# A decoder layer on one core: one load queue with x's first chunk ahead, whole rows of the adaLN weights, sums of squares on TensorE

## The chip, the core and the metric

The kernel runs on one core of a Trainium2 chip. TensorE multiplies, VectorE, ScalarE and GpSimd work on tiles in SBUF and PSUM, and each engine runs its own instructions in the order in which they were emitted. DMAs are issued by SyncE, ScalarE or GpSimd; a queue issues in order, and all share 16 DMA engines. The metric is the device time of one execution in microseconds, the median of several; one execution is profiled.

## The reference

One layer of a decoder for two groups of requests that share weights: a prompt of 1024 tokens, and 8 samples of 8 new tokens each with a paged cache of 4096. D is 1024, all is float32.

```python
mod = (jax.nn.silu(c) @ w_ada + b_ada)[:, None, :]
shift1, scale1, gate1, shift2, scale2, gate2 = jnp.split(mod, 6, axis=-1)
h = rms_norm(x, norm1) * (1 + scale1) + shift1
z = h @ w_in
...
k_cmp = rms_norm(compress(full[:, :, 0], cmp_pe[0], cmp_w1[0], cmp_w2[0]), k_gain[0])
v_cmp = compress(full[:, :, 1], cmp_pe[1], cmp_w1[1], cmp_w2[1])
o_cmp, p_cmp = cmp_attention(q, k_cmp, v_cmp, q_pos)
...
x = x + gate1 * (jnp.concatenate([o_attn, y_conv, y_pool], axis=-1) @ w_out)
h = rms_norm(x, norm2) * (1 + scale2) + shift2
x = x + gate2 * swiglu(h, w_up, w_down)
```

`compress` takes blocks of 32 raw keys or values with a step of 16, adds a position term, and applies a first weight, silu and a second weight. `c` is one vector for the prompt and one for each sample. The change edits how `mod`, the first `h` and the order of the first `compress` calls come about, not what is computed.

## The kernel before

Features lie on the 128 partitions, in KT = 8 tiles; the 1088 tokens (1024 of the prompt, then 64 of the samples) lie along the free axis in three chunks of 384, 384 and 320 (`CHUNKS`). Products of token data and weights are made from parts: an operand is split into `hi` and `lo`, and `mm3` (L142) issues three matmuls.

The program has three phases. **Phase 1** holds
- `ada_rounds` (L339): the six vectors of `mod`. Vectors 0 (shift) and 1 (scale) come first, from 32 loads (`wada`, 256 KB each, 16 buffers); vectors 2 to 5 come late, among the projection (`late_ada`, L899). A step takes 4 loads and 16 fp32 matmuls; a vector's half is then copied (`ada_s`), transposed and added to the bias.
- `norm_load`, `norm_squares`, `modulate` (L435, L441, L404) for each chunk: load of x, sum of its squares, then `h_hi` and `h_lo`. ScalarE makes the squares, VectorE adds the eight tiles, one fp32 matmul with `mean_d` sums over the partitions.
- `token_part` (L672): 9 token tiles by 24 matmuls with the 280 columns of `wtok`. It needs all 8 tiles of its chunk's `h`.
- `input_projection` (L833): 16 tiles of 128 output columns, each three chunks by 24 matmuls. Tiles kc and vc come first, q0 to q3 last; `head_norm` (L700) takes the keys and queries through a mean of squares (`h_sq`, `mean_h`), a root on ScalarE and a reciprocal on VectorE.
- `compress` (L498) for the sample caches: a batch has 4 octets of 8 pages; an octet is 8 loads of 128 KB in a `stream` tile and 16 matmuls, each two records in the trace. There are three `stream` tiles (L475); the first holds the first compression weights for good, two turn, and octet i+2 is loaded when octet i is done. `compress_post` (L575) closes a batch: silu, second weights (`c_w`), norm. The first three batches (EARLY) are spawned with phase 1; the other 20 octets run in phase 2.
- `compress_prompt` (L549): the same for the prompt's 1024 tokens, from `kcv`. ScalarE copies them into a `stream` tile in eight pieces; it waits for the three early batches.

`key_stacks` (L903) then splits the prompt's keys into `kh` (ScalarE) and `kl` (VectorE), from the 64 compressed keys (`kcp`) and the 1024 raw ones (`ksw`). **Phase 2** is attention with the rest of the compression, **phase 3** the output projection and the FFN.

What sets the order: tasks are generators with a priority; `run` (L83) emits the next step of the task with the least priority number among those whose time has come by a rough clock that the code keeps for each engine (`use`, L73). A change of costs, holds or priorities can so reorder all engines far behind it. In `build` (L1951) the front and the projection have priority 1, the early compression 2.

In before, SyncE's queue carries `wada`, the compression weights and the cache pages; ScalarE's queue x and `wtok`.

Of the kernel before, what the change touches and what calls it, by code (L numbers as in the profile page):

```python
# [17 lines left out]
P = 128  # L18
# [42 lines left out]
class Kernel:  # L61
# [84 lines left out]
    def evac(self, out, in_, n, ready=None):  # L146
        """PSUM to SBUF on the engine that is free first; the time at which it is there"""
# [7 lines left out]
    def combine(self, out, a, b, op, n, ready=0.0, eng=None):  # L155
        """out = a op b in SBUF on VectorE or GpSimd, by default the one that is done first"""
# [25 lines left out]
    # ---------------------------------------------------------------- constants  # L182
# [60 lines left out]
    def constants3(self, c):  # L243
        nc = self.nc
        with self.pool("ctmp") as tp:
# [9 lines left out]
            # zeros, then the causal triangle; the window's older edge; the compressed blocks that are not over yet  # L255
# [15 lines left out]
            # row index -> token t of a sample row (b2, g, r, t)  # L271
# [7 lines left out]
            # sum over the four heads of a key group  # L279
# [12 lines left out]
            # new tokens: key (b', t') is seen by row (b, t) when b' == b and t' <= t  # L292
# [11 lines left out]
            # the oldest window keys: key k is out of the window of token t when k <= t  # L304
# [6 lines left out]
            # token partition (64 + (b, t)) -> row (b2, g, r, t) of the pair p  # L311
# [8 lines left out]
            # head of a sample row  # L320
# [10 lines left out]
    # ---------------------------------------------------------------- adaLN  # L331
# [7 lines left out]
    def ada_rounds(self, pool, rs, bufs, eng, tag, margin=0.0):  # L339
        """vectors rs of the modulation, [feature, (prompt, 8 batches)], half a vector at a time"""  # L340
        nc = self.nc
        todo = [(r, hf) for r in rs for hf in range(2)]
        steps = [(x, kh) for x in range(len(todo)) for kh in range(2)]
        W = {}

        def load(i):
            if i < len(steps):
                x, kh = steps[i]
                r, hf = todo[x]
# [9 lines left out]
        for i in range(ahead):  # L359
            load(i)  # L360
        for i, (x, kh) in enumerate(steps):
            r, hf = todo[x]
            yield W[i][4] + margin
            if kh == 0:
# [7 lines left out]
            if kh == 0:  # L372
                continue
            s = pool.tile([P, P], F32, name="ada_s", bufs=2)
            r_ = self.evac(s, acc[:, :P], P)
# [3 lines left out]
            self.tr(tr[:, :P], s)  # L379
            nc.vector.tensor_tensor(  # L380
                self.mod[:, r].rearrange("p (g j) b -> p j g b", j=2)[:, hf],
                tr[:, :P].rearrange("p (g m) -> p g m", m=32)[:, :, 0:9],
                self.bada[:, r].rearrange("p (g j) -> p j g", j=2)[:, hf][:, :, None].to_broadcast([P, 4, 9]),
                op=OP.add)
            self.give(tag, self.use("dve", 0.2, self.t["pe"]))
            if hf == 1:
                if r in (1, 4):
                    out, norm = (self.s1, self.norm1) if r == 1 else (self.s2, self.norm2)
                    nc.vector.scalar_tensor_tensor(out, self.mod[:, r], 1.0, norm[:, :, None].to_broadcast([P, KT, 9]),
                                                   op0=OP.add, op1=OP.mult)  # L390
                self.ada_at[r] = self.use("dve", 0.3, self.t["pe"]) + 0.2
# [1743 lines left out]
```

## Time and profile before

| | us |
|---|---|
| median of 3 runs | 1713.56 |
| the runs | 1712.5, 1713.56, 1716.59 |
| span of the profiled execution | 1707.9 |
| TensorE busy | 1606.5 |
| VectorE busy | 1121.0 |
| ScalarE busy | 821.8 |
| GpSimd busy | 704.6 |

The span runs from the first to the last instruction of one execution; the run's time holds some microseconds around it. A row of a timeline is a run of like instructions with its start, its length, and in brackets how long the engine idled ahead of it and what released it. A group's row has a count, the busy time and the mean of one. Matmuls overlap in the records, so that a mean of 0.29 us stands for starts 0.13 us apart.

### The profile page before, as it was taken

How to read it: one execution, taken by the hardware profiler on the slowest of the kernel's cores; microseconds unless marked ns; L12 is line 12 of the kernel's file. 1: busy time of each engine (PE TensorE's matmuls, PEld its weight loads, DVE VectorE, ACT ScalarE, POOL GpSimd, SP SyncE). 2: the span in 40 equal slices, each digit the busy share in tenths (PEclk: the TensorE clock that was granted, in tenths of full speed). 3: DMA queues.
4: the chain of work that ended last, by engine and by line, in shares of the span. 5: the costliest groups of instructions: out<-in, count | busy, mean ns of one | idle time of the engine just before them, and what ended most of it. 6: DMA issues, size and time to landing. Idle time of an engine off the chain costs nothing.

```text
span 1707.9 us, 35277 instructions
## 1 busy us (share of the span) xinstructions
PE 1606.5 (94%) x12317; PEld 1427.7 (84%) x12317; DVE 1121.0 (66%) x2886; ACT 821.8 (48%) x1892; POOL 704.6 (41%) x812
## 2 busy tenths in 40 slices
PE   6789999997999999999799789999999999899998
PEld 5689999987877566666599779999999998889997
DVE  1491334767556867666599996555555556998887
ACT  1363212326676766766675543332333334655554
POOL 1121000003342322222206486555555555888976
PEclk9899999999999999999999989999999999999999
DMA  9854455425664644540883224225222225744433
GB/s 273 258 180 127 143 141 138 136 75 179 202 193 128 195 141 122 160 131 10 276 253 105 75 72 135 96 96 194 97 96 100 96 96 186 237 128 130 133 82 125
DMA packets 214851, 245.13 MB, mean 144 GB/s; under 512 B 25985, under 2 KB 182850, under 8 KB 214354
## 3 DMA queue, kind: packets, MB, share of 16 engines
q1 hardware_dynamic: 190546, 209.77, 40.1%
q10 hardware_dynamic: 18288, 17.01, 3.2%
q0 software_dynamic: 5840, 16.10, 2.9%
q8 instruction: 98, 1.61, 0.4%
q14 instruction: 79, 0.65, 0.1%
HBM read 202.33 MB, written 44.67 MB: 145 GB/s over the span
## 4 chain that ended last, share of the span: by engine, by line
PE 31%; DVE 9%; issue 4%; DMA 3%; POOL 3%; ACT 1%; ACTq 0%; POOLq 0%; DVEq 0%; SPq 0%
PE bank L135 31%; DVE w_lo L160 2%; DMA w_raw<-in_wup 2%; POOL w_s L160 1%; DVE b_lo L160 1%; DVE g_lo L160 1%; DVE x L1706 1%; DVE d_lo L160 1%; POOL b_t L160 1%; DMA w_raw<-in_wdown 0%; DMA mixc<-mix_d 0%; ACT w_hi L164 0%; DMA x<-x_d 0%; DVE n_ss L160 0%; POOL f_T L160 0%
## 5 line engine op out<-in xcount | busy, mean ns | idle before, releaser
L135 PE MATMUL bank<-b_lo,w_hi 128*128 128x272 f32 x1232 | 355.8, 291 | 2.7 <-DVE b_lo L160 2.5
L135 PE MATMUL bank<-b_hi,w_hi 128*128 128x272 f32 x1232 | 351.6, 292 | 6.9 <-DVE f_v L1512 3.3
L135 PE MATMUL bank<-b_hi,w_lo 128*128 128x272 f32 x1232 | 351.4, 290 | 2.1 <-DVE w_lo L160 2.1
L135 PEld LDWEIGHTS bank<-b_hi,w_hi 128*128 128x128 f32 x1232 | 232.1, 191 | 9.6 <-ACT b_hi L164 4.9
L135 PEld LDWEIGHTS bank<-b_lo,w_hi 128*128 128x128 f32 x1232 | 234.5, 190 | 4.0 <-DVE b_lo L160 3.9
L135 PEld LDWEIGHTS bank<-b_hi,w_lo 128*128 128x128 f32 x1232 | 233.0, 190 | 3.1 <-DVE w_lo L160 2.8
L160 POOL TENSOR_TENSOR w_s<-w_raw 128x512 f32<-128x512 f32 (+1 forms) x122 | 164.2, 1347 | 147.8 <-DVE w_lo L160 134.1
L1011 POOL TENSOR_SCALAR P<-P,st 128x640 f32<-128x640 f32 (+11 forms) x192 | 111.5, 591 | 241.8 <-DVE st L1009 89.5
L164 ACT ACTIVATE w_hi<-w_raw 128x512 fp32r<-128x512 f32 (+2 forms) x130 | 86.5, 676 | 176.5 <-PE bank L135 141.2
L160 DVE TENSOR_TENSOR w_lo<-w_raw,w_hi 128x512 fp32r<-128x512 f32 (+2 forms) x129 | 115.6, 904 | 83.2 <-PE bank L135 47.4
L160 DVE TENSOR_TENSOR w_lo<-w_s,w_hi 128x512 fp32r<-128x512 f32 (+1 forms) x144 | 127.4, 888 | 45.4 <-ACT w_hi L164 38.6
L135 PE MATMUL bank<-stream 128*128 128x128 f32 x1056 | 137.2, 289 | 19.4 <-DMA stream<-in_cacheA 14.5
L135 PEld LDWEIGHTS bank<-stream 128*128 128x128 f32 x1056 | 130.4, 203 | 28.5 <-issue 21.8
L160 POOL TENSOR_TENSOR x<-x,d_m 128x272 f32<-128x272 f32 x144 | 141.1, 1001 | 25.2 <-DVE x L1706 13.1
L164 ACT ACTIVATE w_hi<-w_s 128x512 fp32r<-128x512 f32 (+1 forms) x144 | 89.2, 624 | 113.2 <-PE bank L135 57.1
L135 PE MATMUL bank<-h_hi,w_hi 128*128 128x384 f32 (+1 forms) x384 | 129.4, 337 | 1.0 <-ACT py L826 1.0
L135 PE MATMUL bank<-h_hi,w_lo 128*128 128x384 f32 (+1 forms) x384 | 126.7, 330 | 0.0
L135 PE MATMUL bank<-h_lo,w_hi 128*128 128x384 f32 (+1 forms) x384 | 126.4, 329 | 0.0
L1003 ACT ACTIVATE P<-P,st 128x640 f32<-128x640 f32 (+11 forms) x192 | 113.0, 591 | 13.0 <-DVE st L994 6.5
L135 PE MATMUL bank<-g_hi,w_hi 128*128 128x272 f32 x308 | 92.0, 301 | 13.1 <-DVE x L1706 6.7
L139 PEld LDWEIGHTS bank<-ident,P 128*128 128x128 f32 (+1 forms) x592 | 64.1, 138 | 46.4 <-issue 30.2
L139 PE MATMUL bank<-ident,P 128*128 128x128 f32 (+1 forms) x592 | 95.6, 284 | 2.5 <-DVE pt L152 1.7
(363 smaller groups left out, 4111.0 us busy)
## 6 DMA issues: line engine op xcount, KB each, us to landing
wada<-in_wada SPq DMA_DIRECT2D x96, 256.0 KB, 5.2
stream<-in_cacheA SPq DMA_DIRECT2D x192, 128.0 KB, 3.1
w_raw<-in_wup SPq DMA_DIRECT2D x48, 512.0 KB, 3.9
g_raw<-g_d SPq DMA_DIRECT2D x70, 272.0 KB, 3.1
unit<-in_cacheB SPq DMA_DIRECT2D x136, 128.0 KB, 2.3
stream<-in_cacheB SPq DMA_DIRECT2D x120, 128.0 KB, 2.2
w_raw<-in_wout SPq DMA_DIRECT2D x24, 512.0 KB, 4.5
g_d<-f_T SPq DMA_DIRECT2D x84, 136.0 KB, 1.8
```

Of the source, the lines that this page charges most:

```text
L135: self.nc.tensor.matmul(out, lhsT, rhs, start=start, stop=stop, skip_group_check=chain)
L139: self.nc.tensor.transpose(out, in_, self.ident)
L160: (self.nc.vector if eng == "dve" else self.nc.gpsimd).tensor_tensor(out, a, b, op=op)
L164: self.nc.scalar.activation(hi, src, AF.Copy)
L1003: nc.scalar.activation(Ps, Ps, AF.Exp, scale=-1.0, bias=sy[:, 0:1], accum_out=sy[:, 1:2])
L1011: nc.gpsimd.tensor_scalar(Ps, Ps, sy[:, 3:4], 0.0, op0=OP.mult, op1=OP.add)
L1706: nc.vector.scalar_tensor_tensor(out[:, :n], acc[:, :n], self.mod[:, 5, m, 0:1], out[:, :n], op0=OP.mult, op1=OP.add)
```

## The change

- **Loads.** `x` goes to SyncE's queue: chunk 0 first, then the 32 adaLN loads, `wtok` in two loads (into `stream` tiles), chunk 1 (into the memory of the prompt's keys, `kv_`), chunk 2, then the compression weights and the pages. `issue_after` sets an order of issue only.
- **adaLN.** A load takes two k tiles by 256 columns, so that each row is 2 KB where it was 512 B; a step is 8 matmuls of 256 columns instead of 16 of 128; vector 1 is made before vector 0; a vector is copied once and transposed twice. This holds for the late vectors too.
- **Squares.** TensorE sums them: 8 matmuls with `mean_d` for a chunk, accumulated, in place of VectorE's additions and one matmul (`norm_scale`).
- **Modulation** is made in x's own memory, in two passes over the 8 tiles; the 64 sample tokens are done for all tiles at once.
- **Token weights** are split in two pieces of 4 x 280 columns, the low part on GpSimd.
- **Order.** The compression begins when all of x has been asked for (`x_loaded`), with a priority of 0.9 while the octets lag behind the projection and 2 else; the projection is begun when the early adaLN loads are all issued.
- `ksw` and `kcv` become halves of one tile `kv_`.

```diff
 def ada_rounds(self, pool, rs, bufs, eng, tag, margin=0.0):
-        todo = [(r, hf) for r in rs for hf in range(2)]
-        steps = [(x, kh) for x in range(len(todo)) for kh in range(2)]
+        steps = [(r, kq) for r in rs for kq in range(4)]
...
-                    t = pool.tile([P, KT // 2, P], F32, name="wada", bufs=bufs)
-                    eng.dma_start(t, self.i["wada"][r * 4 + g, :, kh * 4:kh * 4 + 4, hf * P:(hf + 1) * P])
+                    t = pool.tile([P, 2, 256], F32, name="wada", bufs=bufs)
+                    self.ada_load = eng.dma_start(t, self.i["wada"][r * 4 + g, :, kq * 2:kq * 2 + 2, :])
...
-        for i in range(ahead):
-            load(i)
+        with self.tc.issue_after(self.x_load.ins):
+            for i in range(ahead):
+                load(i)
...
-            for k in range(4):
+            for k in range(2):
                 for g in range(4):
-                    self.mm(acc[32 * g:32 * g + 32, :P], self.sc[:, kh * 4 + k, :], W[i][g][:, k, :],
-                            kh + k == 0, kh + k == 4)
+                    self.mm(acc[32 * g:32 * g + 32, 0:256], self.sc[:, kq * 2 + k, :], W[i][g][:, k, :],
+                            kq + k == 0, kq + k == 4)
...
+    def norm_load(self, c, x):
+        c0, n = CHUNKS[c]
+        self.x_load = self.nc.sync.dma_start(x, self.i["xT"][:, :, c0:c0 + n])
+        return x, self.use("dma", n * 4096 / 380e3, self.t["pe"]) + 2.0
+    def norm_scale(self, pool, c, rs, x, r, tag="b"):
...
+        yield from self.hold(lambda: c < 2 or 1 in self.rs)
         m = yield from self.bank_of(tag)
-        self.mm(m[:, :n], self.mean_d, ss[:, :n], True, True)
-        rs = pool.tile([P, 384], F32, name="n_rs", bufs=3)
+        for k in range(KT):
+            sq = pool.tile([P, 384], F32, name="n_t", bufs=2)
+            nc.scalar.activation(sq[:, :n], x[:, k, :n], AF.Square)
+            r = self.use("act", 0.09 + n * 0.00084, r, table="silu") + 0.2
+            yield r
+            self.mm(m[:, :n], self.mean_d, sq[:, :n], k == 0, k == KT - 1)
         nc.scalar.activation(rs[:, :n], m[:, :n], AF.Sqrt, bias=self.eps[:, 0:1])
...
     def compress(self, pool, batches, ahead):
-        yield from self.hold(lambda: self.ada_loaded >= 5)
+        yield from self.hold(lambda: self.x_loaded)
...
+    def token_loads(self):
+        for half in range(2):
+            raw = self.stream_tile().rearrange("p a b -> p (a b)")[:, 0:1120].rearrange("p (k m) -> p k m", k=4)
+            self.nc.sync.dma_start(raw, self.i["wtok"][:, half * 4:half * 4 + 4])
+            self.wt_raw.append((raw, self.use("dma", 1.5, self.t["pe"]) + 2.0))
     def token_part(self, pool, h):
-        for k in range(KT):
-            raw = pool.tile([P, 280], F32, name="wt_raw", bufs=3)
-            nc.scalar.dma_start(raw, self.i["wtok"][:, k])
-            r = self.split(hi[:, k], lo[:, k], raw, 280, self.use("dma", 0.45, self.t["pe"]) + 2)
+        yield from self.hold(lambda: self.wt_raw)
+        for half, (raw, at) in enumerate(self.wt_raw):
+            s = slice(half * 4, half * 4 + 4)
+            yield at
+            r = self.split(hi[:, s], lo[:, s], raw, 1120, at, "pool")
...
     def input_projection(self, h):
-        yield from self.hold(lambda: self.ada_done)
+        yield from self.hold(lambda: self.ada_loaded >= 8)
...
     def front(self, h):
...
+                begin(np_, 0, lambda: np_.tile([P, KT, CHUNKS[0][1]], F32, name="x0"))
+                for t in self.ada_rounds(ap, (1, 0), 16, nc.sync, "b"):
+                    if self.ada_loaded >= 8 and 1 not in xs:
+                        x1 = self.kv.rearrange("p v t -> p (v t)")[:, 0:KT * CHUNKS[1][1]]
+                        with self.tc.issue_after(self.ada_load.ins):
+                            self.token_loads()
+                            begin(np_, 1, lambda: x1.rearrange("p (k t) -> p k t", k=KT))
+                    yield t
...
-        self.run((1, self.front(h)), (1, self.input_projection(h)), (2, self.compress(cp, range(EARLY), 1)))
+        early = lambda: 0.9 if self.octets * 48 < EARLY * 4 * self.z_steps else 2
+        self.run((1, self.front(h)), (1, self.input_projection(h)), (early, self.compress(cp, range(EARLY), 1)))
```

SyncE's queue at the start of the program, before (`in_w` are the first compression weights, `in_cacheA` a page of a sample's cache):

```order
L195 DMA pt<-in_ptab 1x256
L353 DMA wada<-in_wada 128x4x128 x20
L454 DMA stream<-in_w 128x2048
L484 TENSOR_LOAD pt
L488 ISA
L488 DMA stream<-in_cacheA 128x256
```

and after:

```order
L195 DMA pt<-in_ptab 1x256
L405 DMA x_148<-in_xT 128x8x384
L351 DMA wada<-in_wada 128x512 x32
L695 DMA stream<-in_wtok 128x1120 x2
L405 DMA kv__93<-in_xT 128x8x384
L405 DMA x_354<-in_xT 128x8x320
L474 DMA stream<-in_w 128x2048
L504 TENSOR_LOAD pt
L508 ISA
L508 DMA stream<-in_cacheA 128x256
```

The adaLN loads stand together, x and the token weights have come between them and the compression's loads.

TensorE from the early adaLN to the first token matmul, before (`ident` marks a transpose, `n_ss` a chunk's sum of squares, `ksq` and `vcT` a batch's closing):

```order
L135 MATMUL bank<-wada,sc 32x128 x32
L139 MATMUL bank<-ident,ada_s 128x128
L135 MATMUL bank<-n_ss,mean_d 128x384 x2
L135 MATMUL bank<-stream 128x128 x56
L135 MATMUL bank<-vt,c_w_82 64x256 x4
L135 MATMUL bank<-stream 128x128 x8
L135 MATMUL bank<-n_ss,mean_d 128x320
...
L135 MATMUL bank<-stream 128x128 x61
...
L135 MATMUL bank<-wt_hi,h_hi_99 128x280
```

and after, from the end of the adaLN and, behind chunk 0's token tiles, from the position terms (`c_peT`):

```order
L135 MATMUL bank<-wada,sc 32x256 x32
L139 MATMUL bank<-ident,ada_s 128x128 x2
L135 MATMUL bank<-n_t,mean_d 128x384
L135 MATMUL bank<-wt_hi,h_hi_98 128x280
...
L135 MATMUL bank<-c_peT,stream 128x2 x16
L135 MATMUL bank<-n_t,mean_d 128x384 x2
L135 MATMUL bank<-stream 128x128 x32
L135 MATMUL bank<-n_t,mean_d 128x320 x2
L135 MATMUL bank<-stream 128x128 x16
...
L135 MATMUL bank<-vt,c_w_82 64x256 x4
L135 MATMUL bank<-wt_hi,h_hi_100 128x280
```

The token part of chunk 0 has come to stand directly behind the adaLN, five octets behind it, and the other chunks' token tiles behind those.

TensorE behind the last projection matmul, before (`h_sq` a query's squares, `kh` and `qs` the first scores):

```order
L135 MATMUL bank<-h_hi_103,w_lo 128x320
L139 MATMUL bank<-ident,ada_s 128x128
L135 MATMUL bank<-h_sq,mean_h 128x320
L135 MATMUL bank<-stream 128x128 x48
L135 MATMUL bank<-kh_3726,qs 128x192
```

and after:

```order
L135 MATMUL bank<-h_hi_102,w_lo 128x320
L135 MATMUL bank<-ksq,mean_h 128x256
L135 MATMUL bank<-h_sq,mean_h 128x384
L139 MATMUL bank<-ident,vcT 128x128 x2
L135 MATMUL bank<-stream 128x128 x5
L135 MATMUL bank<-h_sq,mean_h 128x320
L135 MATMUL bank<-vt,c_w_82 64x64 x4
L135 MATMUL bank<-ksq,mean_h 128x64
L139 MATMUL bank<-ident,vcT 64x128
L135 MATMUL bank<-stream 128x128 x32
L135 MATMUL bank<-kh_3425,qs 128x192
```

The prompt's compression (the `stream` x5 and the 64 x 64 matmuls) and the third batch's closing have moved behind the projection; the octets ahead of the first scores are two instead of three, and stand behind both.

## Rows read from the trace of the kernel before

**Rows 1.** The page of the profiled execution: its first line, TensorE's share (busy us, share of the span, instructions, then the other engines), TensorE's busy tenths in 40 slices of 42.7 us, and GpSimd's row of its largest group, with us busy and mean ns of one, then idle time ahead and its releaser.
```profile
span 1707.9 us, 35277 instructions
...
PE 1606.5 (94%) x12317; PEld 1427.7 (84%) x12317; DVE 1121.0 (66%) x2886; ACT 821.8 (48%) x1892; POOL 704.6 (41%) x812
...
PE   6789999997999999999799789999999999899998
...
L160 POOL TENSOR_TENSOR w_s<-w_raw 128x512 f32<-128x512 f32 (+1 forms) x122 | 164.2, 1347 | 147.8 <-DVE w_lo L160 134.1
```

**Rows 2.** Busy time of each engine in windows of 10 us: start and end, length, then busy us (and count) of PE, PEld, DVE, ACT and POOL, granted TensorE clock, busy share of the DMA engines, GB/s.
```profile
20.00:30.00 10.00, 5.65 (x64) 3.45 (x62) 0.20 (x1) 0.28 (x1) 0.00 (x0) 1.00 1.07 338
...
60.00:70.00 10.00, 5.06 (x38) 4.64 (x37) 5.40 (x3) 3.69 (x7) 1.07 (x2) 0.94 0.95 306
...
110.00:120.00 10.00, 10.00 (x86) 9.90 (x85) 9.69 (x25) 5.64 (x12) 1.63 (x4) 1.00 0.68 211
```

**Rows 3.** TensorE's waits from 0 to 130 us: who waited, for what, us in total, times, longest.
```profile
PE bank L135 <- DMA wada<-in_wada: 12.6, 11, 4.6
PE bank L135 <- DMA stream<-in_cacheA: 12.1, 4, 4.9
PE bank L135 <- DMA stream<-in_w: 2.7, 1, 2.7
PE bank L135 <- ACT vt L579: 2.2, 1, 2.2
```

**Rows 4.** TensorE's timeline between 28 and 149 us: start, length, operation, out<-in, count of records, idle time ahead with its releaser.
```profile
29.90 6.95 PE L135 MATMUL bank<-c_peT,stream 128*128 128x2 f32 x32 [2.72 <-DMA stream<-in_w]
36.72 6.06 PE L135 MATMUL bank<-stream 128*128 128x128 f32 x32
...
50.50 1.92 PE L135 MATMUL bank<-wada,sc 128*32 128x128 f32 x26
...
59.15 1.46 PE L135 MATMUL bank<-n_ss,mean_d 128*128 128x384 f32 x4
60.45 3.73 PE L135 MATMUL bank<-stream 128*128 128x128 f32 x32
...
113.02 0.38 PE L139 MATMUL bank<-ident,vcT 128*128 128x128 f32 x2
113.16 0.37 PE L135 MATMUL bank<-wt_hi,h_hi 128*128 128x280 f32 x1
113.37 0.29 PE L135 MATMUL bank<-wt_lo,h_hi 128*128 128x280 f32 x1
113.50 0.29 PE L135 MATMUL bank<-wt_hi,h_lo 128*128 128x280 f32 x1
...
128.38 0.66 PE L135 MATMUL bank<-vt,c_w 64*64 64x256 f32 x8 [2.15 <-ACT vt L579]
...
148.24 0.34 PE L135 MATMUL bank<-h_hi,w_hi 128*128 128x384 f32 x1
```

**Rows 5.** TensorE's groups from 0 to 150 us, each shape apart: the octets (records, busy us, mean ns, idle ahead).
```profile
L135 PE MATMUL bank<-stream 128*128 128x128 f32 x384 | 53.6, 303 | 13.0 <-DMA stream<-in_cacheA 12.1 <-DVE n_t L429 0.9
```

**Rows 6.** TensorE's timeline from the end of the projection to the first scores.
```profile
381.01 0.31 PE L135 MATMUL bank<-h_hi,w_lo 128*128 128x320 f32 x1
...
386.05 9.04 PE L135 MATMUL bank<-stream 128*128 128x128 f32 x64 [3.39 <-DVE q L714]
397.08 3.81 PE L135 MATMUL bank<-stream 128*128 128x128 f32 x32 [2.00 <-DMA stream<-in_cacheA]
400.65 0.34 PE L135 MATMUL bank<-kh,qs 128*128 128x192 f32 x1
```

**Rows 7.** VectorE's timeline in the same place: a reciprocal of the queries, a key difference, the queries' low part.
```profile
383.25 2.15 DVE L713 RECIPROCAL h_sq<-h_sq 128x320 f32<-128x320 f32 x1
...
388.53 1.22 DVE L918 TENSOR_TENSOR kl<-ksw,kh 64x1024 fp32r<-64x1024 f32 x1
...
399.88 2.84 DVE L944 TENSOR_TENSOR qs<-q,qs 64x512 fp32r<-64x512 f32 x4
```

**Rows 8.** Three windows of the first 34 us, columns as in Rows 2: adaLN loads alone, then with x's first two chunks among them.
```profile
12.00:18.00 6.00, 4.23 (x39) 2.11 (x43) 0.47 (x3) 0.28 (x1) 0.00 (x0) 1.00 1.17 302
24.00:28.00 4.00, 2.72 (x33) 1.80 (x33) 0.20 (x1) 0.28 (x1) 0.00 (x0) 1.00 0.99 382
28.00:34.00 6.00, 4.10 (x20) 4.13 (x20) 0.00 (x0) 0.00 (x0) 0.00 (x0) 1.00 1.07 370
```

**Rows 9.** ScalarE's groups from 0 to 382 us, each shape apart: the first token operand, the prompt's copies for the compression, table loads of the compression's activation.
```profile
L421 ACT ACTIVATE h_hi<-n_t,mod 128x384 fp32r<-128x384 f32 x16 | 9.5, 610 | 0.7 <-DVE n_t L419 0.5
L150 ACT ACTIVATE stream<-kcv 64x512 f32<-64x512 f32 x7 | 7.7, 1104 | 0.1
...
L579 ACT ACT_TABLE_LOAD x4 | 5.1, 1283 | 2.3 <-DVE pre L577 2.3
```

**Rows 10.** TensorE's groups from 150 to 380 us, each shape apart: the late adaLN matmuls.
```profile
L135 PE MATMUL bank<-wada,sc 128*32 128x128 f32 x512 | 18.8, 276 | 0.0
```

**Rows 11.** ScalarE's timeline at the end of phase 1: the last copy of the 64 compressed keys, the first of the 1024 raw ones.
```profile
385.02 0.26 ACT L916 ACTIVATE kh<-kcp 64x64 fp32r<-64x64 f32 x1
385.29 1.06 ACT L914 ACTIVATE kh<-ksw 64x1024 fp32r<-64x1024 f32 x1
```

**Rows 12.** A window of 10 us behind the last projection, columns as in Rows 2.
```profile
380.00:390.00 10.00, 6.19 (x33) 5.41 (x32) 9.73 (x27) 7.53 (x15) 5.88 (x22) 0.83 0.01 2
```

More of the change, by code (lines that the diff above doesn't have):

```diff
@@ L378, in ada_rounds @@
             tr = yield from self.bank_of(tag)
[L379 to L391, printed above, removed]
+            for j in range(2):
+                self.tr(tr[:, j * P:(j + 1) * P], s[:, j * P:(j + 1) * P])
+            for j in range(2):
+                nc.vector.tensor_tensor(
+                    self.mod[:, r].rearrange("p (g j) b -> p j g b", j=2)[:, j],
+                    tr[:, j * P:(j + 1) * P].rearrange("p (g m) -> p g m", m=32)[:, :, 0:9],
+                    self.bada[:, r].rearrange("p (g j) -> p j g", j=2)[:, j][:, :, None].to_broadcast([P, 4, 9]),
+                    op=OP.add)
+            self.give(tag, self.use("dve", 0.4, self.t["pe"]))
+            if r in (1, 4):
+                out, norm = (self.s1, self.norm1) if r == 1 else (self.s2, self.norm2)
+                nc.vector.scalar_tensor_tensor(out, self.mod[:, r], 1.0, norm[:, :, None].to_broadcast([P, KT, 9]),
+                                               op0=OP.add, op1=OP.mult)
+            self.ada_at[r] = self.use("dve", 0.3, self.t["pe"]) + 0.2
     def square_sum(self, pool, ss, x, k, n, ready, width=384, eng="dve"):
@@ new lines, in norm_scale, with modulate @@
+        self.rs[c] = rs, self.use("dve", n * 0.0066 + 0.1, r)
+    def modulate(self, c, x, hi, lo, at):
+        nc = self.nc
+        c0, n = CHUNKS[c]
+        s, sh = self.s1, self.mod[:, 0]
+        yield from self.hold(lambda: c in self.rs and 1 in self.ada_at)
+        rs, r = self.rs[c]
+        np_ = min(n, SEQ - c0)
+        yield max(r, self.ada_at[1]) - 0.5
+        if np_ < n:
+            r3 = lambda a: a.rearrange("p k (b t) -> p k b t", t=NT)
+            v = x[:, :, np_:n]
+            nc.vector.tensor_tensor(v, v, rs[:, None, np_:n].to_broadcast([P, KT, n - np_]), op=OP.mult)
+            nc.vector.tensor_tensor(r3(v), r3(v), s[:, :, 1:9][:, :, :, None].to_broadcast([P, KT, NB, NT]), op=OP.mult)
+            self.use("dve", 1.3)
+        for k in range(KT):
+            t = x[:, k, :np_]
+            nc.vector.scalar_tensor_tensor(t, t, s[:, k, 0:1], rs[:, :np_], op0=OP.mult, op1=OP.mult)
+            self.use("dve", n * 0.00107 + 0.15)
+        yield from self.hold(lambda: 0 in self.ada_at)
+        yield self.ada_at[0] - 0.3
+        for k in range(KT):
+            t = x[:, k, :np_]
+            hk, lk = hi[:, k, :np_], lo[:, k, :np_]
+            nc.scalar.activation(hk, t, AF.Identity, bias=sh[:, k, 0:1])
+            r = self.use("act", 0.22 + n * 0.001)
+            nc.vector.scalar_tensor_tensor(lk, t, sh[:, k, 0:1], hk.bitcast(F32), op0=OP.add, op1=OP.subtract)
+            at[k] = self.use("dve", n * 0.00107 + 0.15, r) + 0.1
@@ L432, in modulate @@
             if k % 2:
                 yield self.t["dve"] - 1.0
[L435 to L446 removed]
+        if np_ < n:
+            nc.vector.tensor_tensor(r3(v), r3(v), sh[:, :, 1:9][:, :, :, None].to_broadcast([P, KT, NB, NT]), op=OP.add)
+            r = self.use("dve", 0.7)
+            hk, lk = hi[:, :, np_:n], lo[:, :, np_:n]
+            nc.scalar.activation(hk, v, AF.Copy)
+            r = self.use("act", 0.6, r)
+            nc.vector.tensor_tensor(lk, v, hk.bitcast(F32), op=OP.subtract)
+            at[:] = [self.use("dve", 0.7, r) + 0.1] * KT
@@ L453, in compress_setup @@
         self.w1 = w1
-        nc.sync.dma_start(w1, self.i["w1"].rearrange("p v k m -> p (v k) m"))
-        for x in range(2):
-            self.compress_load(x)
+        with self.tc.issue_after(self.x_load.ins):
+            nc.sync.dma_start(w1, self.i["w1"].rearrange("p v k m -> p (v k) m"))
+            for x in range(2):
+                self.compress_load(x)
         yield self.use("dma", 2.9, self.t["pe"]) + 2.5
@@ L1920, in front, with begin @@
     def front(self, h):
+        nc = self.nc
+        self.rs = {}
+        xs = {}
+        def begin(pool, c, x):
+            rs = pool.tile([P, 384], F32, name="n_rs", bufs=2)
+            xs[c] = self.norm_load(c, x())
+            self.spawn(0.4 + 0.1 * c, self.norm_scale(pool, c, rs, *xs[c]))
+            self.spawn(0.4 + 0.1 * c, self.modulate(c, xs[c][0], h[c][0], h[c][1], self.h_at[c]))
         with self.pool("norm") as np_:
@@ L1973, in build @@
         kp = kp_.__enter__()
[L1974 to L1975 removed]
+        self.kv = kp.tile([P, 4, T], F32, name="kv_")
+        self.ksw, self.kcv = self.kv[:, 0:2], self.kv[:, 2:4]
         self.kcp = kp.tile([P, 64], F32, name="kcp")
```

74 lines of the change are left out of this document (14 added, 60 removed).

## The prediction

> **What bounds the kernel now.** I read the page first, then the windows, the waits and the timeline of TensorE in the stretch that the change edits, and last the place where that stretch hands over to attention. TensorE is busy for 94% of the span, and its busy tenths are 9 nearly everywhere except in the first three slices, in slice 9 (384 to 427 us), around slice 22 and at the end [rows 1]. So only time in which TensorE idles, or runs at its lower clock, can be won, and the change edits one such place, the first 128 us.
>
> There the windows show TensorE busy 5.65 us of 10 from 20 us, 5.06 from 60, and full from 110 [rows 2]. The waits say why: 12.6 us for adaLN weights, 12.1 us for octets of the sample caches, 2.7 us for the compression weights and 2.2 us for the compression's activation [rows 3]. The timeline shows a second cost: at 36.72 us an octet takes 6.06 us, at 60.45 the same 32 records take 3.73, and the compression's position terms at 29.90 take 6.95 us, so TensorE ran at the lower of its levels until about 41 us. The first token matmul is at 113.16, the first projection matmul at 148.24, and by then [rows 4] 12 octets of the three early batches are done, 384 records of 32 each [rows 5].
>
> At the other end of phase 1 the last projection piece ends at 381.3 us. TensorE idles 3.39 us, runs two octets, idles 2.00 us, runs a third, and begins the prompt's scores at 400.65, 19.3 us behind the last projection [rows 6]. What ends last there is VectorE: it finishes the low parts of the keys and then the low part of the queries, begun at 399.88 [rows 7]. Any work that the new order puts into that chain is paid for at once.
>
> **The new loads.** All go on one queue: x0 (1.57 MB), 32 adaLN pieces (8.39 MB), token weights (1.15 MB), x1, x2, then compression weights and octets. In before the adaLN loads alone, in pieces of 512 B, moved 302 GB/s at a busy share of 1.17; when x's rows of 1536 B were among them the windows show 382 and 370 [rows 8]. The new adaLN rows have 2 KB. I take 375 GB/s: 9.96 MB in 26.6 us, and with 4 us before the first bytes (the first adaLN wait of before was 4.6 [rows 3]) the last piece lands at 30.6 us. The other end, 302 GB/s, is 37 us.
> The Trainium skill, DMA: Bandwidth & Descriptors (Specifications), says that pieces of 512 B and more already go at line rate, and gives 358 GB/s as the HBM limit of a core. By its limit, as an estimate, the loads would end 1.2 us later and the sum be 1718; the trace passed it with 382 in one window, so I don't use it. Its 512 B rule is a rival below.
>
> **From the last load to dense work.** The last adaLN step at the low clock costs 2 us (26 records took 1.92 [rows 4]), its copy, transposes and additions about 1.5: modulation is ready at 34. Eight h_hi of 0.61 us follow on ScalarE, each with its low part behind it on VectorE [rows 9]: 39.5. I take TensorE as dense from 40.5. The low half of the token weights is now GpSimd's: 1347 ns for 512 columns [rows 1] is 2.95 us for each of two pieces of 1120, which may cost up to 3 us more for the first token tile. The squares for chunk 0 are hidden in the loading time; they cost nothing on TensorE there, which waits for weights anyway.
>
> **TensorE's work until the first projection**, in the new order:
> - token part, 216 matmuls: 9.2 us for 72 by starts 0.128 us apart (0.13 from 113.37 to 113.50 [rows 4]): 27.7 in all
> - squares of chunks 1 and 2, 16 fp32 matmuls, each with 2 records: two took 1.46 us [rows 4], so 8 x 0.73 + 8 x 0.6 = 10.6; in before this was VectorE's work
> - position terms at full clock, half of 6.95: 3.5
> - 10 octets of 3.73 (60.45 [rows 4]): 37.3
> - the closing of two batches, 0.66 for the second weights, 0.38 for transposes [rows 4] and some 0.5 for the means, 1.5 each: 3
> - waits: 5, for the low clock at the start and one reload of the octet buffers; bounds 0, and 15, about the waits of before for octets, compression weights and activation, with 12.1 + 2.7 [rows 3]
>
> Together 87.1, so the first projection stands at 127.6 instead of 148.24. But 2 octets and one closing (9.0) are still owed, so the gain is 11.6 us and not 20.6.
>
> **The rest of phase 1.** Before took 233.1 us from first to last projection (148.24 to 381.3), with no waits over 1 us. After adds 9.0 for what is owed. Late adaLN has the same columns in half as many matmuls: the old 512 records took 18.8 us [rows 10]; 256 columns in one matmul save some start cost, 0 to 3.7, and I take 2. The prompt's compression is moved to the last tiles: eight copies of 1.10 us each [rows 9] now stand on ScalarE among the squares that free TensorE's banks; in before they ran while TensorE was full. They cost 0 to 8.8; I take 2.5, since TensorE still has other tiles' work. Some 2 us of the prompt's matmuls fall behind the last projection. Sum: 127.6 + 233.1 + 9.0 - 2 + 2.5 - 2 = 368.2, against 381.3.
>
> **The handover.** The new order has, behind the last projection piece, the second half of the prompt's compression, its four matmuls with the second weights, and only then two octets and the first scores. On ScalarE the eight key copies of 1.06 us (from 385.29 [rows 11]) now stand ahead of that compression's evacuation, and on VectorE its addition stands behind the reciprocals, the key differences (1.22 each [rows 7]) and their casts. VectorE was busy 9.73 of 10 us in this place in before [rows 12]; the 18 us of its queue there, from the last projection to the queries at 399.88 [rows 7] without the 64-column keys, plus 3.5 for the last batch's reciprocal (2.15 us for 320 columns [rows 7]), copies and scaling, reach the addition 21 us behind the last projection. Then, each waiting for the last: table load (1.28 [rows 9]) and activation 1.8, second weights 0.7, squares and their mean 1, table load and root 1.9, reciprocal and scaling 0.7, eight key copies of 0.26 [rows 11] and their low parts 2.5, queries' low part 1.4: about 10 to 11. So the first scores come 32 us behind the last projection instead of 19.3; bounds 26 and 36. TensorE stands nearly empty from 3 us behind the projection until 24, while the octets which could have filled it are queued behind the waiting matmuls of the prompt. Two octets run there instead of three, so one more is owed: 3.7.
>
> **Sum.** 368.2 + 32 = 400.2 for the first scores, plus 3.7 owed: 403.9 against 400.65, that is +3.3. Behind it TensorE is nearly full for 400 us, so I carry this to the end: 1707.9 + 3.3 = 1711.2 for the span, and with 5.7 us between this span and the median of 1713.56, **1717 us**. That is within 0.3% (5.1 us), about the least that a measurement of this kernel tells from no change.
>
> **Rivals.**
> 1. The handover costs less (faster). The scores were VectorE's to release in before too, and if the prompt's closing finds its place between VectorE's casts, the scores come 24 us behind the projection, 8 less; with 2.5 for the copies and 1.5 of waits not paid: 1705. For it: the chain's members are short. Against: engines run in order, and the addition stands behind the casts in the row.
> 2. The octets starve TensorE (slower). Five octets now stand nearly back to back behind chunk 0's tokens, and their loads are last in the queue, in two buffers that turn, since the third holds the compression weights. Before had four such waits with 12.1 us in all [rows 3]. If four come on top of the wait that I count, 9 to 12 us, I take 10: 1727. It decides where a reload takes longer than TensorE's work between. Against it: an octet of 1.05 MB needs 2.8 us at 375 GB/s and TensorE 3.73 for it.
> 3. The longer rows bring nothing (slower), so that the change doesn't do what it says. The loads go at 302 GB/s, dense work starts 6.5 us later: 1723. This is what the Trainium skill's 512 B rule would have here; 382 against 302 GB/s in the windows speaks against it.
>
> **Chances.** Forecast 0.47, rival 1 0.22, rival 2 0.20, rival 3 0.11. The forecast's own range, from half of the bounds each way, is 1709 to 1723; a part of it, 0.07, lies over 1718.7. Faster by over 0.3%: 0.22. Within: 0.40. Slower: 0.20 + 0.11 + 0.07 = 0.38. The range to hold 8 in 10 reaches to rivals 1 and 2: 1703 to 1729.
>
> **What would show it.** Right: the last early adaLN load lands near 30 us and the first token matmul starts near 40; the first projection matmul between 122 and 134; the last projection piece near 368; TensorE idle for some 20 us behind it, with ScalarE's activation of the prompt's compression and the four small matmuls with the second weights about 23 us behind; first scores near 400. Wrong: the prompt's matmuls done before the keys' copies (rival 1); waits for cache loads over 10 us between 60 and 125 (rival 2); under 320 GB/s between 8 and 30 us (rival 3). A shift of the later slices by more than the handover's difference would say that phase 2's order matters, which I price at nothing.

## The result and the profile after

The changed kernel takes 1735.02 us (median, 1734.49 to 1739.19) against 1713.03: ratio 1.0135, 95% interval 1.0107 to 1.0163. It is slower by 22 us; the forecast was 1717, the range ended at 1729. Its profiled execution has a span of 1732.9 us.

The page (its first line, busy us by engine, and busy tenths and granted clock of TensorE in 40 slices) shows what the mean hides, since TensorE's share fell only from 94% [rows 1] to 93%:

```profile
span 1732.9 us, 34470 instructions
...
PE 1616.5 (93%) x11975; PEld 1419.8 (82%) x11975; DVE 1108.0 (64%) x2822; ACT 819.8 (47%) x1877; POOL 709.2 (41%) x814
...
PE   5999999975989899999899889999999999989998
...
PEclk9899999987999999999999989999999999999999
```

The first slice is emptier, the next are full, and slices 8 and 9 (347 to 433 us) fall to 7 and 5. Four windows that end at the first projection matmul, the last one, the first scores and the end of phase 2 tell how the time is spread (columns as in [rows 2]). Before:

```profile
0.00:148.24 148.24, 115.74 (x934) 101.56 (x935) 73.97 (x187) 57.52 (x125) 26.19 (x54) 0.94 0.74 223
148.24:381.32 233.08, 231.63 (x1767) 217.20 (x1765) 104.32 (x138) 60.05 (x103) 14.52 (x25) 1.00 0.46 128
381.32:400.65 19.33, 13.53 (x100) 12.74 (x99) 18.52 (x51) 13.86 (x22) 8.00 (x26) 0.91 0.35 110
400.65:836.80 436.15, 423.85 (x3203) 286.70 (x3201) 287.49 (x1395) 300.73 (x789) 132.09 (x229) 1.00 0.51 156
```

After:

```profile
0.00:132.71 132.71, 108.60 (x773) 86.10 (x773) 54.19 (x117) 51.18 (x99) 29.02 (x51) 0.94 0.71 235
132.71:376.48 243.77, 241.67 (x1562) 218.39 (x1561) 105.29 (x139) 58.47 (x98) 15.64 (x27) 0.99 0.41 122
376.48:410.16 33.68, 12.24 (x94) 11.18 (x93) 27.43 (x65) 19.38 (x34) 8.49 (x27) 0.70 0.24 74
410.16:862.50 452.34, 431.07 (x3235) 293.88 (x3233) 284.57 (x1387) 301.70 (x795) 132.93 (x231) 0.98 0.51 154
```

The first projection comes 15.5 us earlier, with two octets fewer; the last is 4.8 us ahead of before; the handover takes 33.7 us instead of 19.3; and phase 2 takes 16.2 us more, of which 7.2 is more TensorE time and 9.0 is idling. What is behind it differs by 0.7. TensorE's timeline of after at the front and the handover (it answers to [rows 4] and [rows 6]):

```profile
33.92 3.00 PE L135 MATMUL bank<-wada,sc 128*32 128x256 f32 x14 [1.58 <-DMA wada<-in_wada]
...
44.05 1.65 PE L135 MATMUL bank<-n_t,mean_d 128*128 128x384 f32 x2 [5.92 <-ACT n_t L417]
44.92 1.01 PE L135 MATMUL bank<-wt_hi,h_hi 128*128 128x280 f32 x1
...
400.57 0.49 PE L135 MATMUL bank<-vt,c_w 64*64 64x64 f32 x8 [21.13 <-DVE pre L529]
401.37 0.69 PE L135 MATMUL bank<-ksq,mean_h 128*128 128x64 f32 x2 [0.31 <-ACT ksq L614]
...
410.16 0.34 PE L135 MATMUL bank<-kh,qs 128*128 128x192 f32 x1
...
427.29 9.40 PE L135 MATMUL bank<-stream 128*128 128x128 f32 x64 [5.28 <-DMA stream<-in_cacheA]
...
484.69 1.12 PE L135 MATMUL bank<-pt,vt__285 128*64 128x256 f32 x4 [4.34 <-ACT pt L150]
```

The gap of 21.13 us is the one forecast, and ScalarE's timeline names its end: the activation of the prompt's compression, with the table load ahead of it, stands behind the key copies and waits 9.77 us for VectorE's addition (L597).

```profile
387.40 1.05 ACT L943 ACTIVATE kh<-kv__93 64x1024 fp32r<-64x1024 f32 x1
...
398.69 1.28 ACT L599 ACT_TABLE_LOAD   x1 [9.77 <-DVE pre L597]
```

The second gap, 5.28 us ahead of 427.29, wasn't forecast. SyncE's queue explains it: it stood 22.9 us on TensorE, since a page can be loaded only when an octet's buffer is free; then one octet's pages went out, behind them 16 loads of phase 2's own, and only at 421.13 the next octet's:

```profile
406.86 2.93 SPq L508 DMA_DIRECT2D stream<-in_cacheA  x6
410.46 9.26 SPq L508 DMA_DIRECT2D unit<-in_cacheB  x16
421.13 7.67 SPq L508 DMA_DIRECT2D stream<-in_cacheA  x12
```

In before the queue stood 19.4 us at the same place, but then 18 pages went out ahead of the same 16 loads:

```profile
391.55 12.29 SPq L488 DMA_DIRECT2D stream<-in_cacheA  x18
404.51 10.12 SPq L488 DMA_DIRECT2D unit<-in_cacheB  x16
```

Three windows of after, columns as in [rows 2], show the loads' rate behind 28 us and the granted clock (third number from the end) around the two later gaps: 0.57 and 0.66, so part of the time at the lower of the two levels. Before has such a stretch in phase 2 too (0.83 from 414 to 424 us); over the whole of phase 2 it was granted 1.00, after 0.98.

```profile
28.00:36.00 8.00, 6.24 (x65) 2.63 (x66) 6.31 (x12) 0.00 (x0) 0.00 (x0) 0.97 1.04 393
...
420.00:432.00 12.00, 6.49 (x33) 6.03 (x33) 4.01 (x40) 3.07 (x14) 2.10 (x6) 0.57 0.59 176
480.00:490.00 10.00, 5.66 (x29) 4.64 (x28) 5.44 (x30) 6.55 (x22) 3.50 (x9) 0.66 0.86 256
```

### The profile page after: what moved, and what is told of

Read it like the earlier page. It is cut to its first block, busy times and chain, and to the rows that moved or that the text cites. A ratio compares the mean times of both kernels' runs of the same rounds, so it can differ in the third digit from the quotient of the medians.

```text
span 1732.9 us, 34470 instructions
## 1 busy us (share of the span) xinstructions
PE 1616.5 (93%) x11975; PEld 1419.8 (82%) x11975; DVE 1108.0 (64%) x2822; ACT 819.8 (47%) x1877; POOL 709.2 (41%) x814
## 4 chain that ended last, share of the span: by engine, by line
PE 67%; DVE 12%; DMA 7%; issue 6%; POOL 4%; ACT 3%; SPq 1%; ACTq 0%; POOLq 0%; DVEq 0%
PE bank L135 61%; PE bank L139 5%; DVE w_lo L160 2%; DMA w_raw<-in_wup 2%; POOL w_s L160 1%; DVE x L1733 1%; DVE g_lo L160 1%; DVE b_lo L160 1%; DMA stream<-in_cacheA 1%; DVE d_lo L160 1%; SPq L508 1%; POOL b_t L160 1%; DMA w_raw<-in_wdown 1%; DVE n_ss L160 1%; POOL x L160 1%
## 5 line engine op out<-in xcount | busy, mean ns | idle before, releaser
L1038 POOL TENSOR_SCALAR P<-P,st 128x128 f32<-128x128 f32 (+10 forms) x192 | 111.3, 590 | 240.5 <-DVE st L1036 111.2
L135 PE MATMUL bank<-stream 128*128 128x128 f32 x1056 | 133.7, 284 | 9.8 <-DMA stream<-in_cacheA 9.2
L1030 ACT ACTIVATE P<-P,st 128x128 f32<-128x128 f32 (+10 forms) x192 | 113.0, 590 | 21.7 <-DVE st L1021 14.2
L139 PEld LDWEIGHTS bank<-ident,P 128*128 128x128 f32 (+1 forms) x592 | 62.6, 137 | 50.0 <-issue 34.6
```

The source lines that it names most:

```text
L135: self.nc.tensor.matmul(out, lhsT, rhs, start=start, stop=stop, skip_group_check=chain)
L139: self.nc.tensor.transpose(out, in_, self.ident)
L1030: nc.scalar.activation(Ps, Ps, AF.Exp, scale=-1.0, bias=sy[:, 0:1], accum_out=sy[:, 1:2])
L1038: nc.gpsimd.tensor_scalar(Ps, Ps, sy[:, 3:4], 0.0, op0=OP.mult, op1=OP.add)
```

## The experiments

Theory A: the front gains, and the loss is made at the handover, where the prompt's closing stands behind the keys, and is passed on to phase 2. Theory B: the front itself costs, by TensorE's additional work and lower clock, and the handover only moves octets.

**Octets due at twice the rate** in the changed kernel:

```diff
-        early = lambda: 0.9 if self.octets * 48 < EARLY * 4 * self.z_steps else 2
+        early = lambda: 0.9 if self.octets * 24 < EARLY * 4 * self.z_steps else 2
```

> The changed kernel with one constant different: the early octets are due at twice the rate (the test has 24 in place of 48), so that the third batch and with it the prompt's compression are closed in the middle of the projection and not behind it. Theory A (the loss is made at the handover: the prompt's closing stands behind the key copies and casts, TensorE is empty for 21 us, and phase 2 inherits late loads): first scores about 20 us behind the last projection instead of 33.7, three octets ahead of them; 1735 minus 14 minus 4 for the octet, and up to 12 less in phase 2: 1705 to 1717. Theory B (the loss is TensorE's additional work and lower clock at the front; the handover only moves octets): the octets merely run earlier, within 5 us of 1735.

1712.33 us, ratio to before 0.9998 (0.9979 to 1.0017): 22.7 us faster than the changed kernel by one constant. Its timeline:

```profile
373.67 1.49 PE L135 MATMUL bank<-h_sq,mean_h 128*128 128x384 f32 x4
380.18 9.41 PE L135 MATMUL bank<-stream 128*128 128x128 f32 x64 [5.02 <-DVE q L741]
392.04 3.81 PE L135 MATMUL bank<-stream 128*128 128x128 f32 x32 [2.45 <-DMA stream<-in_cacheA]
395.60 0.34 PE L135 MATMUL bank<-kh,qs 128*128 128x192 f32 x1
```

No prompt's closing stands there, three octets do, and the scores come 21.8 us behind the last projection. Phase 2 takes 440.1 us instead of 452.3. Of the 23.7 us between the two profiled executions 11.9 are the handover's and 12.2 phase 2's; the last projection ends 2.7 us earlier, and what is behind phase 2 takes 3.1 more. Theory A holds in that where the prompt is closed carries the loss; how it gets into phase 2 is open here. The constant matters because the octets' pace is spread over all 48 projection pieces, so that the third batch, for which the prompt's compression waits, ended with the projection.

**Rows of 512 B** in the changed kernel, each load as two:

```diff
-                    self.ada_load = eng.dma_start(t, self.i["wada"][r * 4 + g, :, kq * 2:kq * 2 + 2, :])
+                    for j in range(2):
+                        self.ada_load = eng.dma_start(t[:, :, j * P:(j + 1) * P],
+                                                      self.i["wada"][r * 4 + g, :, kq * 2:kq * 2 + 2, j * P:(j + 1) * P])
```

> The changed kernel with each adaLN load issued as two loads of 512 B rows; nothing else differs, the order of all engines' work is the same. If the longer rows carry the faster front: the last early adaLN load lands some 6 us later than 33.9 us, the first projection starts 4 to 6 us later than 132.7, and the time is 1739 to 1742. If the rows bring nothing (the token weights and x's second chunk decide when dense work begins): landing within 2 us, time within 2 us of 1735.

1749.94 us (ratio 1.0220, 1.0199 to 1.0241), 15 more than the changed kernel. Window of 12 to 28 us, this kernel first, the changed kernel second:

```profile
12.00:28.00 16.00, 15.00 (x78) 4.72 (x77) 1.31 (x3) 5.80 (x10) 0.00 (x0) 1.00 0.95 256
```

```profile
12.00:28.00 16.00, 14.27 (x78) 4.75 (x78) 1.67 (x5) 5.80 (x10) 0.00 (x0) 1.00 0.97 341
```

The busy share is about the same, the rate 256 GB/s against 341. The first token matmul comes at 54.4 instead of 44.9 and the first projection 10.6 us later: more than the 4 to 6 expected. Here the loads are also twice as many and half as large, so the 10 us are for both together. Most of the rest of the 15 us lies in phase 2, which takes 459.6 instead of 452.3 although nothing was changed there; no run says why.

**Squares on VectorE** in the changed kernel (`rs` takes the sum):

```diff
...
-            self.mm(m[:, :n], self.mean_d, sq[:, :n], k == 0, k == KT - 1)
+            if k:
+                r = self.combine(rs[:, :n], rs[:, :n], sq[:, :n], OP.add, n, r, "dve")
...
+        self.mm(m[:, :n], self.mean_d, rs[:, :n], True, True)
```

> The changed kernel with VectorE adding the eight squares again and one matmul for each chunk. Its plan also closes the prompt's compression before the last projection, so it is to be set against the first kernel of this set. If the squares cost TensorE their length: 21 fp32 matmuls fewer, some 10 us of which 5 were hidden in the loading, so 5 to 9 us faster than the first kernel. If VectorE then holds up the tokens of chunks 1 and 2: no faster than the first kernel, or slower by up to 5.

1704.14 us, ratio to before 0.9952 (0.9934 to 0.9971). The last projection ends at 373.2, in the kernel with octets at twice the rate at 373.8, both with the same octets done. But the pace of the octets differs as well (12 are done at the first projection here, 10 there), so no run shows the squares' price alone. The 8 us between the medians lie behind: scores 19.7 us behind the projection instead of 21.8, phase 2 436.1 instead of 440.1, and the rest 870.6 instead of 873.5. The squares aren't in those stretches, so the size that was expected came for another reason.

**Late prompt in the kernel before**:

```diff
-        yield from self.hold(lambda: self.cmp_done == EARLY)
+        yield from self.hold(lambda: self.cmp_done == EARLY and self.z_steps >= 47)
```

> The kernel before with one hold more: the prompt's compression waits until 47 of the 48 projection pieces are emitted, so its closing falls behind the last projection; two octets ahead of the scores instead of three. Its addition on VectorE still stands ahead of the key differences and casts. If lateness of the prompt alone makes the loss: first scores 30 us or more behind the last projection, time 1725 or more. If it is the place behind the key copies and casts that costs: scores 20 to 25 us behind, time 1713 to 1719.

1723.34 us, ratio 1.0052 (1.0032 to 1.0071): between the two expectations in size. The four matmuls with the second weights come 1 us behind the projection, as VectorE's addition stands ahead of the keys, but the compressed keys and the queries' low part come last there, and TensorE waits:

```profile
383.73 0.34 PE L135 MATMUL bank<-vt,c_w 64*64 64x64 f32 x8
386.69 0.69 PE L135 MATMUL bank<-ksq,mean_h 128*128 128x64 f32 x2 [2.61 <-ACT ksq L594]
...
404.34 0.53 PE L135 MATMUL bank<-kh,qs 128*128 128x192 f32 x1 [8.32 <-DVE qs L944]
...
405.31 6.17 PE L135 MATMUL bank<-stream 128*128 128x128 f32 x32
...
474.26 1.12 PE L135 MATMUL bank<-pt,vt__610 128*64 128x256 f32 x4 [4.34 <-ACT pt L150]
```

The scores are only 21.9 us behind the projection: with the prompt's closing late too, but its addition ahead of the keys, the handover isn't long. There are two octets ahead of them, though, and phase 2 takes 450.2 us instead of 436.2. It does so without late loads: SyncE's queue sends the pages and the 16 loads ahead of the scores, and TensorE waits for no octet's page in phase 2.

```profile
392.34 3.56 SPq L488 DMA_DIRECT2D stream<-in_cacheA  x6
396.64 9.23 SPq L488 DMA_DIRECT2D unit<-in_cacheB  x16
```

What it shares with the changed kernel is the wait of 4.34 us for ScalarE's copy `pt`, and an octet at the lower clock (6.17 us) behind a wait. The profiled execution is 17.0 us longer than before's, more than the medians differ; 2.6 of that are the handover's, 14.0 phase 2's, with the octet that it got. Up to the first projection, where nothing was changed, it is 3.0 us longer: so much one execution can differ from another.

**Keys behind the prompt's activation** in the changed kernel (in `key_stacks`; `prompt_silu` is that activation, kept in `compress_post`, which isn't shown):

```diff
-                    with self.tc.issue_after(self.last_scale.ins), self.tc.issue_after(self.last_sqrt.ins):
+                    with self.tc.issue_after(self.last_scale.ins), self.tc.issue_after(self.prompt_silu.ins):
```

> The changed kernel with the key copies issued behind the activation of the prompt's compression; TensorE's order is the same row for row, only ScalarE's and VectorE's order at the handover differs. If the queue order makes the gap: the four matmuls with the second weights come 6 to 10 us behind the last projection instead of 24, TensorE's gap of 21 us falls to under 8 and a second one opens ahead of the scores, the octets' next loads start some 14 us earlier and the later gap of 5.3 us is gone; time 1722 to 1730. If the amount of VectorE's work decides alone: scores still 33 us behind the projection, the gap only changes place, within 3 us of 1735.

1734.72 us: no gain. The scores come 31.6 us behind the projection, as the second theory had it, and the gap ahead of a page stays (5.76 us at 424.71). The first gap was only cut in two, for the squares of the closing (L616) still stood behind the key copies on ScalarE:

```profile
389.54 0.49 PE L135 MATMUL bank<-vt,c_w 64*64 64x64 f32 x8 [10.79 <-DVE pre L529]
397.98 0.69 PE L135 MATMUL bank<-ksq,mean_h 128*128 128x64 f32 x2 [7.95 <-ACT ksq L616]
```

**Keys behind the whole closing**: the same with `self.prompt_root`, the closing's root, as the mark.

> The changed kernel with the key copies issued behind the whole closing of the prompt's compression (its root on ScalarE), so that TensorE gets through that closing early; TensorE's row is the same up to there, and the plan now puts a third octet ahead of the first scores. In the changed kernel SyncE's queue waited 22.9 us for those octets and no load moved meanwhile. If phase 2's additional waits are inherited from that held queue and the octet owed: octets about 391 to 399 us instead of 402 to 410, the next loads 12 us earlier, the 5.3 us gap behind the first scores gone, one octet less in phase 2, which shortens by 8 to 12 us; scores still 30 to 34 us behind the projection (VectorE); time 1722 to 1728. If phase 2's order itself is the cause and not the held loads: phase 2 shorter by the octet alone, 1729 to 1733.

1722.38 us, ratio 1.0070 (1.0036 to 1.0104), 12.6 less than the changed kernel, as the first theory in that expectation had it:

```profile
387.83 0.49 PE L135 MATMUL bank<-vt,c_w 64*64 64x64 f32 x8 [10.79 <-DVE pre L529]
...
389.68 9.96 PE L135 MATMUL bank<-stream 128*128 128x128 f32 x64
...
402.29 5.25 PE L135 MATMUL bank<-stream 128*128 128x128 f32 x32 [2.52 <-DMA stream<-in_cacheA]
407.29 0.34 PE L135 MATMUL bank<-kh,qs 128*128 128x192 f32 x1
```

The scores are 33.2 us behind the projection, about as in the changed kernel; VectorE ends the queries' low part at 404.8, and the third octet, late by its pages, keeps TensorE until 407.29. But the octets lie in the gap, a third fits, and phase 2 takes 442.4 us: 9.9 us less. Two things changed here at once, one octet less in phase 2 and earlier loads; the late prompt in the kernel before, with early loads and an octet owed, has the long phase 2 all the same. So the octet owed, and not the held loads alone, goes with the long phase 2.

**The adaLN part alone in the kernel before**: `ada_rounds` of the changed kernel, with its long rows and its matmuls of 256 columns, everything else as it was.

> The kernel before with the change's adaLN part alone: 2 KB rows, 8 matmuls of 256 columns a step, whole vectors; queues, squares and order are before's. If the rows are worth what the 512 B kernel lost (9.5 us at the first token matmul), most of the 12.6 us of waits for adaLN weights go: 1704 to 1709. If the octets' loads, which share the queue in before, wait in their place: within 3 us of 1713.

1707.62 us, ratio 0.9961 (0.9942 to 0.9980). The last projection ends at 374.8, 6.6 us earlier than in before. TensorE still waits 12.4 us for adaLN weights, but the waits for octets fell from 12.1 [rows 3] to 6.3:

```profile
PE bank L135 <- DMA wada<-in_wada: 12.4, 6, 5.1
PE bank L135 <- DMA stream<-in_cacheA: 6.3, 4, 2.6
```

The time is the first expectation's, the reason isn't: the adaLN waits stayed, the octets' went. That the shared queue passed the gain on to the pages is argued, not shown.

**Two queues**: the kernel with squares on VectorE, x and token weights issued by ScalarE.

```diff
-        self.x_load = self.nc.sync.dma_start(x,
+        self.x_load = self.nc.scalar.dma_start(x,
...
-            self.nc.sync.dma_start(raw, self.i["wtok"][:, half * 4:half * 4 + 4])
+            self.nc.scalar.dma_start(raw, self.i["wtok"][:, half * 4:half * 4 + 4])
```

> The third experiment's kernel with x and the token weights back on ScalarE's queue; rows of 2 KB, squares on VectorE. If the single queue's order is worth something of its own: x and token weights (up to 4.2 MB more, 11 us at 375 GB/s) land among the adaLN loads, the last of which comes 5 to 10 us later, and the first projection starts 3 to 8 us later than 140.8; time 1707 to 1712. If only the longer rows carry the gain at the front, and octets fill what TensorE waits: within 3 us of 1704.

1722.87 us, 18.7 more than with one queue; the first projection is 19.3 us later, against 3 to 8 expected. ScalarE now issues the token weights and chunk 1 ahead of chunk 0, which is asked for only at 21.00 us:

```profile
1.37 0.93 ACTq L697 DMA_DIRECT2D stream<-in_wtok  x2
...
3.10 0.62 ACTq L405 DMA_DIRECT2D kv__93<-in_xT  x1
...
21.00 0.57 ACTq L405 DMA_DIRECT2D x<-in_xT  x1
```

TensorE's waits up to the first projection are 17.9 us for adaLN weights, 17.5 for octets and 5.9 for chunk 0's sum:

```profile
PE bank L135 <- DMA wada<-in_wada: 17.9, 14, 6.3
PE bank L135 <- DMA stream<-in_cacheA: 17.5, 7, 6.9
PE bank L135 <- DVE n_rs L160: 5.9, 1, 5.9
```

**Token weights' low half on VectorE too**, on top of the squares there (`"dve"` for `"pool"` in `token_part`).

> The changed kernel with VectorE adding the squares, as in the third experiment, and the low half of the token weights on VectorE too (about 1.3 us for 1120 columns instead of 2.6 to 2.9 on GpSimd). If the 1.3 us that TensorE waited for GpSimd there count: 1 to 2 us faster than the third experiment, 1702 to 1704. If VectorE's h_lo stands behind them in its queue: the same or up to 3 us slower.

1704.58 us, ratio to before 0.9943 (0.9920 to 0.9965): the same as without. This, the kernel with squares on VectorE alone and the adaLN part in the kernel before (0.9961) are the three whose interval lies below the kernel before, by less than 1%.

## Why the prediction was wrong

- **The front** was right in kind. The loads went at 341 GB/s between 12 and 28 us and not 375, the last adaLN step began at 33.9, and TensorE, in its row order, then waited 5.92 us for chunk 1's first square, behind h_hi and the token weights on ScalarE. Dense work began at 44, not 40.5, the first projection at 132.7, not 127.6 (the work between took 88.7 us for 87.1): 5.1 us late, and in the range that the text gave (122 to 134).
- **The rest of phase 1** took 243.8 us for a sum of 240.6. The saving of 2 us on late adaLN didn't come: its 256 records were busy 20.8 us, where 512 had taken 18.8 [rows 10]; in two other kernels with the 256 records (octets at twice the rate, the adaLN part in before) they took 19.0. A wait of 2.1 us for a query's square was new.
- **The handover** was right, place, order and size: 33.7 us for 32 forecast, the gap 21.1 for "some 20", the second weights at 24.1 behind the projection for 23.
- **The sum's last step failed**: "Behind it TensorE is nearly full for 400 us, so I carry this to the end". Phase 2 was given one octet, 3.7 us, and took 16.2; another order in it was priced "at nothing". The other 12.5 are 9.0 of additional idling and 3.5 of longer TensorE time, at a granted clock of 0.98 instead of 1.00. The largest new waits are those of 5.28 us ahead of 427.29 and 4.34 ahead of 484.69; windows around them were granted 0.57 and 0.66. The runs side by side show what phase 2 goes with (early and late: the prompt's compression closed before or behind the last projection; octets: between there and the first scores; scores: us behind the last projection; phase 2 in us):

  | kernel | prompt closed | octets | scores | phase 2 |
  |---|---|---|---|---|
  | before | early | 3 | 19.3 | 436.2 |
  | squares on VectorE | early | 3 | 19.7 | 436.1 |
  | the same, token weights too | early | 3 | 19.7 | 437.9 |
  | the same, two queues | early | 3 | 19.8 | 438.4 |
  | octets at twice the rate | early | 3 | 21.8 | 440.1 |
  | adaLN part in before | early | 3 | 20.3 | 440.8 |
  | keys behind the closing | late | 3 | 33.2 | 442.4 |
  | late prompt in before | late | 2 | 21.9 | 450.2 |
  | changed kernel | late | 2 | 33.7 | 452.3 |
  | keys behind the activation | late | 2 | 31.6 | 453.9 |
  | rows of 512 B | late | 2 | 34.6 | 459.6 |

  Phase 2 goes by the octets ahead of the scores and not by the length of the handover. Among the late kernels one octet owed goes with some 8 to 17 us (442.4 against 450.2 to 459.6), where its own matmuls take 3.7; the late prompt by itself goes with 2 to 6 (442.4 against 436.1 to 440.8). These are single executions, and the late kernels differ in the place of the keys too.
- By terms: 5.1 + 3.2 + 1.7 + 12.5 - 0.7 behind phase 2 = 21.8, the difference between the forecast span of 1711.2 and 1732.9; between this span and the median lie 2.1 us, not the 5.7 that the forecast took over from before. The profiled execution of before was a short one, then: the spans differ by 25.0 us, the medians by 22.0, and some 3 us of the terms above may be its luck.
- **Rivals.** Rival 2 (octets starve TensorE at the front, 10 us) is refuted: waits for octets' pages were 2.6 us up to 150. Rival 3 (long rows bring nothing) too: 341 against 256 GB/s, and 6.6 us in the kernel before by the adaLN part alone. With that the Trainium skill's line in DMA: Bandwidth & Descriptors (Specifications), that 512 B and more go at line rate, isn't borne out here: 256 GB/s with rows of 512 B (in loads of half the size; a window of before had 302 [rows 8]) and 341 with 2 KB. The 358 GB/s that the same section gives as a core's limit was passed too, with 393 in the window of 28 to 36 us. Rival 1 (the handover costs less) is refuted by the 33.7 us; with another constant its handover of 24 us would have been near (21.8), its time of 1705 not (1712.33).
- The wait at 484.69 comes neither from the octet owed nor from the held loads: all five kernels with the late prompt have it, at 4.3 us (in the one with the keys behind the closing at 473.00, in the late prompt of before at 474.26), and in the other six TensorE waits for such a copy at most 1.1 us. It goes with the order of phase 2 that a late prompt leaves.
- What stays open: by which of phase 2's smaller waits an octet of 3.7 us comes with 8 and more, and what the 5.28 us alone are worth; no run moved one of them by itself.

## What to carry to other kernels

A change that makes work at the front denser leaves its filler (here the octets) for later; look where the last of it closes, and who waits for that. Work that is pushed over the border of a stage is not paid by its own length alone: an octet of 3.7 us went with a phase 2 that was some 8 us or more longer, whether the handover ahead of it was long or short. Pace a filler so that it ends well ahead of the next stage, then check the end of the stage in the order of every engine.

## What the runs showed that was not expected

- Two queues cost 19 us at the first projection against one (160.1 against 140.8), with the same bytes. The number of queues alone isn't the reason: with the adaLN part in the kernel before, where x and the token weights are ScalarE's too, the first projection comes at 142.4, with the same 12 octets done. The reading is that the token weights and chunk 1, which were asked for first, were not needed first; no run moved the order alone.
- Half as many matmuls of twice the columns saved nothing in late adaLN: 256 records in 19.0 to 20.8 us, 512 in 18.8.
- 21 fp32 matmuls more on TensorE are not seen at the last projection (373.8 us with them, 373.2 without), although TensorE looked full there. Executions with the same order up to there differ by some 2 to 3 us (first projection at 130.3, 132.7 and 133.6 in the three with other places for the keys), and the octets' pace differs too, so this shows no price and not that there is none.
